# Down-projection weight sums by accumulating DMA, with the final norm out of place

## The chip, the cores and the metric

The kernel runs on one core of one Trainium2 chip, as one program. The metric is the device time of one execution in microseconds (us), given as a median over runs. In the profile the engines are PE (TensorE matmul), PEld (its weight loads), DVE (VectorE), ACT (ScalarE), POOL (GpSimd) and SP (SyncE); SPq is SP's queue of transfers.

## The reference

One decoder layer over 1024 tokens of width 1024 in float32: a mixer with three groups of attention heads, then a gated feed-forward block. The change lies in the last lines only, the down projection, the last norm and the residual:

```python
h = rmsnorm(x, ffn_pre_norm[l])
u = causal_depthwise_conv(h @ w_up[l], conv_w[l], conv_b[l])
gate, up = jnp.split(u, 2, axis=-1)
y = (jax.nn.gelu(gate, approximate=True) * up) @ w_down[l]      # (1024 x 2816) @ (2816 x 1024)
x = x + rmsnorm(y, ffn_post_norm[l])
# rmsnorm(y, g) = y * rsqrt(mean(y*y) + 1e-6) * g
```

## The kernel before

Every float32 product is made of three matmuls: each operand is split into a high part (a cast to float32r on ACT) and the rest (a subtraction on DVE), and high by high, high by rest and rest by high are added in PSUM (`mm3`). A `form` is this split of one operand: one cast on ACT (L935) and one subtraction on DVE (L138) into a tile `wf`.

The down projection is done in 2 x 2 blocks with seven products instead of eight, P1, P2, P7, P5, P6, P3, P4 in this order, each called a pass. A pass runs over 11 pairs `p` of contraction blocks (`ND` = 11); the step for one pair is four row tiles of 128 rows by 512 columns, three matmuls each, so 12 matmuls. Before its step a pair needs two forms: one of the activations (`dg`, read back from `gd` in HBM) and one of the weights (`dwr`, from `w_down`). The passes P7, P5, P6 and P4 need sums of weight blocks: P7 the difference of two blocks, P5 the difference of two others, P6 a block minus the P5 result, P4 a block minus the P6 result. `t_sum` makes these sums on DVE (L906, `dwr<-dwr`), and the sums of P5 and P6 are kept in HBM (`td`) for the passes after.

The order on PE, DVE, ACT and POOL is written by hand: `down_items` is a list of (time, function), sorted by time, with one unit of time for one step, and each engine issues its instructions in this order. SP's order is set by the scheduler from its own estimate of when each transfer may start; SP also issues in order, and a transfer that waits holds up those behind it. In a pass every item leads its step by a fixed number of steps: `w_load` by 4.6, `t_sum` by 2.7, the two forms by 2.2 and 1.8.

After a pass its four PSUM tiles are added into `y` (`evac`). The last pairs of P4 (`TAIL` of them) are ordered by row tile instead of by pair, so that one row tile after another is complete; for each, `evac`, `norm1` and `norm2` follow: DVE adds PSUM to `y`, ACT squares and sums `y` into `dsq`, DVE multiplies `y` by the gain `gff` in place, DVE reduces `dsq` and forms the variance, POOL takes its power -0.5 (L112), DVE scales by it and adds the residual `x2r` (L1282, in two halves), and SP writes the tile out.

Weight tiles of the passes after P1 have the tag `p` with six buffers, shared with the tiles of the phase before.

Of the kernel before, what the change touches and what calls it, by code (L numbers as in the profile page):

```python
# [9 lines left out]
F32 = mybir.dt.float32  # L10
# [3 lines left out]
ALU = mybir.AluOpType  # L14
AX = mybir.AxisListType
# [28 lines left out]
ND = NC2 // 2  # L44
# [3 lines left out]
PB = 6  # L48
# [11 lines left out]
def trunk_kernel(ctx: ExitStack, tc: tile.TileContext, a: dict, out: bass.AP):  # L60

    nc = tc.nc
    V, A, G, T = nc.vector, nc.scalar, nc.gpsimd, nc.tensor

    cst = ctx.enter_context(tc.tile_pool(name="cst", bufs=1))
# [38 lines left out]
    def blk(i, n=P):  # L104
        return slice(i * n, (i + 1) * n)

    def rstd(dst, ssq, n):

        w = ssq.shape[-1]
        v = sm("var", w)  # L110
        V.tensor_scalar(out=v, in0=ssq, scalar1=1.0 / n, scalar2=EPS, op0=ALU.mult, op1=ALU.add)  # L111
        G.tensor_tensor(out=dst, in0=v, in1=mhalf[:, 0:w], op=ALU.pow)  # L112

    def square_sum(dst, src):

# [161 lines left out]
    def step(f, *x):  # L277
        return lambda: f(*x)
# [626 lines left out]
    def tt(eng, out_, x, y, op):  # L905
        eng.tensor_tensor(out=out_, in0=x, in1=y, op=op)  # L906
# [3 lines left out]
    def h2_forms(k2):  # L910

        pairs = {"B11": (0, k2), "B12": (1, k2), "B21": (0, k2 + 2), "B22": (1, k2 + 2)}
        for n, key in pairs.items():
            hB[n, k2] = (h2h[key], h2l[key])
        b11, b12, b21, b22 = (h2r.pop(pairs[n]) for n in ("B11", "B12", "B21", "B22"))
        t1 = S("hf", F32, (P, 2, 512))

        def form(n, x):
            hi, lo = S("hTf", F32R, (P, 2, 512)), S("hTf", F32R, (P, 2, 512))
            A.copy(hi, x)  # L920
            sub(lo, x, hi, V)
# [8 lines left out]
    LO, HI = slice(0, 512), slice(512, 1024)  # L930

    def split(x, eng=None):

        f = S("wf", F32R, (P, 2, 512))
        A.copy(f[:, 0], x)  # L935
        sub(f[:, 1], x, f[:, 0], eng or V)
        return f

    def up_pair(j, at):
# [28 lines left out]
        for n, tm in (("A11", -3.7), ("A12", -2.7), ("S2", -1.7), ("S1", -0.7), ("S3", 0.3), ("S4", 1.6), ("A22", 2.3)):  # L968
            it.append((tm, step(form, n)))
# [172 lines left out]
    for x, i in enumerate(PRE[NAUTO:]):  # L1142
        t0 = 4.0 * (x - NF + NAUTO)
# [33 lines left out]
    def a_of(m, p):  # L1177
        return {"P1": lambda: g1[p][:, LO], "P2": lambda: g2[p][:, LO], "P7": lambda: g1[p][:, LO], "P5": lambda: g1[p][:, HI],
                "P6": lambda: g1[p][:, LO], "P3": lambda: g2[p][:, LO], "P4": lambda: g2[p][:, HI]}[m]()

    def b_of(m, p):
        return wr[m, p][:, HI if m == "P5" else LO]

    def w_load(m, p):
        early = m == "P1"
        t = wr[m, p] = S("dwr", tag="s" if early else "p", bufs=None if early else PB)
        w1, w2 = a["w_down"][p], a["w_down"][ND + p]
        src = {"P1": ((LO, w1[:, LO]),), "P2": ((LO, w2[:, LO]),), "P7": ((LO, w1[:, HI]), (HI, w2[:, HI])),
               "P5": ((slice(0, 1024), w1),), "P6": ((LO, w2[:, HI]), (HI, td[0, p])), "P3": ((LO, w2[:, HI]),),
               "P4": ((LO, w2[:, LO]), (HI, td[1, p]))}[m]  # L1190
        for sl, x in src:
            load(t[:, sl], x)

    def t_sum(m, p):
        t = wr[m, p]
        if m == "P7":
            tt(V, t[:, LO], t[:, HI], t[:, LO], ALU.subtract)
        elif m == "P5":
            tt(V, t[:, HI], t[:, HI], t[:, LO], ALU.subtract)
            load(td[0, p], t[:, HI])  # L1200
        else:
            tt(V, t[:, LO], t[:, LO], t[:, HI], ALU.subtract)
            if m == "P6":
                load(td[1, p], t[:, LO])
# [13 lines left out]
    def form(m, p, side):  # L1218
        forms[m, p, side] = split(b_of(m, p) if side else a_of(m, p))
        if side:  # L1220
            del wr[m, p]
        elif m == "P4":
            del g2[p]

# [43 lines left out]
    def norm1(t, c):  # L1268
        if t not in sqs:
            sqs[t] = cst.tile([P, 2], F32, name=f"dsq{t}")  # L1270
        hs = blk(c, 512)
        square_sum(sqs[t][:, c:c + 1], y[t][:, hs])
        tt(V, y[t][:, hs], y[t][:, hs], env2["g"][:, hs], ALU.mult)

    def norm2(t):
        xt = env2.pop(("x", t))
        s_, r = sm("zs", 1), sm("zr", 1)
        V.tensor_reduce(out=s_, in_=sqs[t], axis=AX.X, op=ALU.add)
        rstd(r, s_, D)
        for c in range(2):  # L1280
            hs = blk(c, 512)
            V.scalar_tensor_tensor(out=y[t][:, hs], in0=y[t][:, hs], scalar=r, in1=xt[:, hs], op0=ALU.mult, op1=ALU.add)  # L1282
            if t == NT - 1:
                load(out[0, blk(t), hs], y[t][:, hs])
        if t < NT - 1:
            load(out[0, blk(t), :], y[t])

    def x_get(t):
        env2["x", t] = S("x2r", tag="pt", bufs=2) if t < 2 else S("x2r")
        load(env2["x", t], x2d[blk(t), :])  # L1290

    TAIL = 3
    down_items = []

    def at_(tm, f, *x):
        down_items.append((tm, step(f, *x)))

    for x, m in enumerate(PASS):
        for p in range(ND):
            t0 = ND * x + p  # L1300
            tf_ = t0
            if x == 6 and p >= ND - TAIL:
                tf_ = ND * x + ND - TAIL + (p - ND + TAIL) / 4
            if m == "P1":
                at_(t0 - 5.6, g_load, p, 0)
            if m == "P2":
                at_(t0 - 6.6, g_load, p, 1)
            at_(tf_ - (5.5 if m == "P1" else 4.6), w_load, m, p)
            if m not in ("P1", "P2", "P3"):
                at_(tf_ - 2.7, t_sum, m, p)  # L1310
            if m == "P2":
                at_(t0 - 1.0, s_sum, "S3", p)
            elif m == "P7":
                at_(t0 - 3.3, s_sum, "S1", p)
            elif m == "P5":
# [122 lines left out]
```

## Time and profile before

| | before |
|---|---|
| median of 3 runs | 1207.08 us (1206.49 to 1207.63) |
| the profiled execution's own time | 1205.29 us |
| its span, first to last instruction | 1203.3 us |
| mean granted TensorE clock in it | 0.983 of full speed |
| PE, DVE, ACT, POOL busy share of the span | 95%, 77%, 48%, 18% |
| transfers | 156.47 MB, all on SP's queue, 39.2% of the 16 engines' span |

The shares are means over a span with many stages. The profiled execution is 1.79 us under the median of the runs, and 1.99 us of its own time lie outside the span.

### The profile page before, as it was taken

Reading aid. Unit: us, or ns where it says so; the run is one execution under the profiler, and the core shown is the slowest. Engines: PE = TensorE matmul, PEld = TensorE weight load, DVE = VectorE, ACT = ScalarE, POOL = GpSimd, SP = SyncE. Lnnn points to the kernel's source line nnn. Section 1 sums busy time; section 2 is a strip of 40 time slices with the busy share of each in tenths; the row PEclk is TensorE's granted clock in tenths of the full one; section 3 lists DMA queues with packets and bytes.
Section 4 is the critical chain, followed back from the end, with each engine's and each line's share of the span. In section 5 each row is a group of like instructions: output and inputs, shape, how many; then the busy total and the mean of one; then the engine's idle time right before and its main releaser. Section 6 shows DMA issues by size and latency. Waiting matters only on the chain.

```text
span 1203.3 us, 15547 instructions
## 1 busy us (share of the span) xinstructions
PE 1142.7 (95%) x5634; PEld 952.3 (79%) x5634; DVE 929.7 (77%) x1422; ACT 581.8 (48%) x1175; POOL 217.2 (18%) x157
## 2 busy tenths in 40 slices
PE   7999989999887999999999999999999999999993
PEld 6977768788776788878888888888888888888872
DVE  6357576765589898762689999989898888896996
ACT  5315543244277777753554434444443455344541
POOL 1100010012077454430001221212122110000000
PEclk9999989999989999999999999999999999999997
DMA  9393224513551222141113212122221489567573
GB/s 345 123 281 89 57 63 159 180 36 106 162 137 36 71 70 87 37 157 35 53 53 123 95 64 105 70 88 83 75 105 59 147 311 340 158 219 249 190 244 140
DMA packets 68462, 156.47 MB, mean 130 GB/s; under 512 B 7169, under 2 KB 23089, under 8 KB 68385
## 3 DMA queue, kind: packets, MB, share of 16 engines
q1 hardware_dynamic: 68384, 155.48, 39.2%
q8 instruction: 44, 0.72, 0.3%
q14 instruction: 34, 0.27, 0.1%
HBM read 116.78 MB, written 37.63 MB: 128 GB/s over the span
## 4 chain that ended last, share of the span: by engine, by line
PE 75%; DVE 13%; DMA 5%; ACT 3%; issue 3%; POOL 1%; SPq 0%; DVEq 0%; POOLq 0%; ACTq 0%
PE p L142 6%; PE p L143 6%; PE p L141 6%; PE scd L620 4%; PE psct L141 3%; PE psct L142 3%; PE psct L143 3%; DVE wf L138 3%; PE xz L142 3%; PE xz L143 3%; PE xz L141 3%; PE accd L653 2%; PE pso L141 2%; PE pso L143 2%; PE pso L142 2%
## 5 line engine op out<-in xcount | busy, mean ns | idle before, releaser
L883 DVE SCALAR_TENSOR_TENSOR u<-C,cw,u 128x1023 f32<-128x1023 f32 (+1 forms) x88 | 112.4, 1279 | 11.5 <-ACT u L880 11.4
L880 ACT ACTIVATE u<-C,cw 128x1024 f32<-128x1024 f32 x44 | 54.8, 1245 | 113.4 <-DVE C L906 88.3
L906 POOL TENSOR_TENSOR sq<-sq,sq 128x512 f32<-128x512 f32 x18 | 29.2, 1622 | 354.5 <-DVE sq L906 354.5
L935 ACT CAST wf<-dwr 128x512 fp32r<-128x512 f32 x77 | 48.0, 623 | 82.1 <-DVE dwr L906 65.0
L141 PE MATMUL p<-h2h,wf 128*128 128x512 f32 x216 | 84.0, 389 | 0.0
L142 PE MATMUL p<-h2l,wf 128*128 128x512 f32 x216 | 84.0, 389 | 0.0
L143 PE MATMUL p<-h2h,wf 128*128 128x512 f32 x216 | 84.0, 389 | 0.0
L653 PE MATMUL accd<-pt,v 128*128 128x256 f32 (+1 forms) x336 | 61.0, 301 | 16.0 <-DVE pt L138 11.6
L630 ACT ACTIVATE pd<-scd,nm 128x128 f32<-128x128 f32 (+3 forms) x64 | 47.5, 743 | 54.4 <-DVE nm L628 49.1
L134 ACT CAST pt<-tpd 128x512 fp32r<-128x512 f32 (+1 forms) x80 | 42.3, 542 | 64.3 <-PE tpd L643 51.6
L141 PE MATMUL psct<-hTh,wh 128*128 128x512 f32 x176 | 69.7, 396 | 0.0
L142 PE MATMUL psct<-hTl,wh 128*128 128x512 f32 x176 | 69.3, 394 | 0.0
L143 PE MATMUL psct<-hTh,wl 128*128 128x512 f32 x176 | 69.0, 392 | 0.0
L653 PEld LDWEIGHTS accd<-pt,v 128*128 128x128 f32 x336 | 50.1, 200 | 22.6 <-DVE pt L138 14.4
L138 DVE TENSOR_TENSOR wf<-wraw,wf 128x512 fp32r<-128x512 f32 x90 | 61.6, 684 | 2.7 <-ACT wf L935 2.7
L138 DVE TENSOR_TENSOR pt<-tpd,pt 128x512 fp32r<-128x512 f32 (+1 forms) x80 | 49.6, 630 | 18.0 <-ACT pt L134 17.6
L138 DVE TENSOR_TENSOR wf<-dwr,wf 128x512 fp32r<-128x512 f32 x77 | 52.7, 685 | 12.8 <-ACT wf L935 12.5
L628 DVE TENSOR_REDUCE nm<-scd 128x1 f32<-128x128 f32 (+3 forms) x64 | 46.9, 750 | 17.7 <-PE scd L620 17.4
L112 POOL TENSOR_TENSOR zr<-var,mhalf 128x1 f32<-128x1 f32 x24 | 13.2, 549 | 260.9 <-DVE var L111 260.9
L141 PE MATMUL xz<-hTf,wf 128*128 128x512 f32 x144 | 56.0, 389 | 0.0
L142 PE MATMUL xz<-hTf,wf 128*128 128x512 f32 x144 | 56.0, 389 | 0.0
L143 PE MATMUL xz<-hTf,wf 128*128 128x512 f32 x144 | 56.0, 389 | 0.0
(291 smaller groups left out, 3502.9 us busy)
## 6 DMA issues: line engine op xcount, KB each, us to landing
wraw<-in_w_up_dram SPq DMA_DIRECT2D x44, 512.0 KB
dwr<-in_w_down_dram SPq DMA_DIRECT2D x77, 256.0 KB
gd<-u SPq DMA_DIRECT2D x22, 512.0 KB
dg<-gd SPq DMA_DIRECT2D x22, 512.0 KB
wraw<-in_wqk_dram SPq DMA_DIRECT2D x11, 512.0 KB
dwr<-in_w_down_dram SPq DMA_DIRECT2D x11, 512.0 KB
td<-dwr SPq DMA_DIRECT2D x22, 256.0 KB
dwr<-td SPq DMA_DIRECT2D x22, 256.0 KB
```

The lines of the kernel that those rows point to most:

```text
L134: A.copy(dst, src)
L138: (eng or G).tensor_tensor(out=dst, in0=x, in1=hi.bitcast(F32), op=ALU.subtract)
L141: T.matmul(ps, lhsT=lh, rhs=rh, start=start, stop=False)
L142: T.matmul(ps, lhsT=lh, rhs=rl, start=False, stop=False)
L143: T.matmul(ps, lhsT=ll, rhs=rh, start=False, stop=stop)
L620: T.matmul(sc[:, off + c0:off + c1], lhsT=ql[0:rows, blk(i)], rhs=kl[0:rows, c0:c1], start=x == 0, stop=x == len(passes) - 1)
L628: V.tensor_reduce(out=nm, in_=s, axis=AX.X, op=ALU.max, negate=True)
L630: A.activation(p[:, 0:n], s, AF.Exp, bias=nm, accum_out=den[:, i, hd["d"]:hd["d"] + 1])
L653: T.matmul(acc[:, cs], lhsT=hd["v"][:, j], rhs=pt[:, x, bs], start=j == 0 and x == 0, stop=d == 1 and x == 1 and (o == len(ops) - 1 or (o ...
L880: A.activation(us[i], ct2[i], AF.Identity, bias=cw[:, i, 3:4], scale=cw[:, i, 2:3])
L883: V.scalar_tensor_tensor(out=us[i][:, d:], in0=ct2[i][:, 0:SEQ - d], scalar=cw[:, i, 2 - d:3 - d], in1=us[i][:, d:], op0=ALU.mult, op1=ALU ...
L935: A.copy(f[:, 0], x)
```

## The change

Weights: a tile `dwr` now holds one block for each of two pairs of steps (512 columns each), so six buffers hold twelve pairs. A sum is no longer made on DVE. The first block is loaded, in P7 and P5 ACT multiplies it by -1 in place (`w_neg`, L1193), and a transfer issued by POOL adds the second block onto it in SBUF (`w_add`, L1197, `accum_op`). P7's sum goes to `td` by SP; P6 starts from it, and after its form ACT negates it and SP stores it for P4 (`w_keep`). The loads of P7, P5, P6 and P4 lead by 7.6 steps, the negations by 6.0, the accumulating transfers by 5.6.

Norm: the product with the gain goes to a new tile `yg` instead of back into `y`; the reduction and the power (`norm_r`) are apart from the last scaling (`norm2`), and stand earlier in the list.

Tail: `TAIL` is 4, so the last four pairs are ordered by row tile.

```diff
     def b_of(m, p):
-        return wr[m, p][:, HI if m == "P5" else LO]
+        return wr[m, p // 2][:, blk(p % 2, 512)]
...
+        load(b_of(m, p), {"P1": w1[:, LO], "P2": w2[:, LO], "P7": w1[:, HI], "P5": w1[:, LO], "P6": td[0, p],
+                          "P3": w2[:, HI], "P4": td[1, p]}[m])
+
+    def w_neg(m, p):
+        A.mul(b_of(m, p), b_of(m, p), -1.0)
+
+    def w_add(m, p):
+        w1, w2 = a["w_down"][p], a["w_down"][ND + p]
+        G.dma_start(out=b_of(m, p), in_={"P7": w2[:, HI], "P5": w1[:, HI], "P6": w1[:, LO], "P4": w2[:, LO]}[m],
+                    accum_op=ALU.add)
         if m == "P7":
-            tt(V, t[:, LO], t[:, HI], t[:, LO], ALU.subtract)
...
+            load(td[0, p], b_of(m, p))
+
+    def w_keep(p):
+        w_neg("P6", p)
+        load(td[1, p], b_of("P6", p))
...
+        if (t, 2) not in y:
+            y[t, 2] = S("yg")
         square_sum(sqs[t][:, c:c + 1], y[t][:, hs])
-        tt(V, y[t][:, hs], y[t][:, hs], env2["g"][:, hs], ALU.mult)
+        tt(V, y[t, 2][:, hs], y[t][:, hs], env2["g"][:, hs], ALU.mult)
...
-    TAIL = 3
+    TAIL = 4
...
-            at_(tf_ - (5.5 if m == "P1" else 4.6), w_load, m, p)
+            at_(tf_ - (5.5 if m == "P1" else 4.6 if m in ("P2", "P3") else 7.6), w_load, m, p)
+            if m in ("P7", "P5"):
+                at_(tf_ - 6.0, w_neg, m, p)
             if m not in ("P1", "P2", "P3"):
-                at_(tf_ - 2.7, t_sum, m, p)
+                at_(tf_ - 5.6, w_add, m, p)
...
-                at_(t0 + 5.2, s_sum, "S4", p)
+                at_(t0 - 1.2, s_sum, "S4", p)
...
-                at_(e0 + 0.07, norm2, t + 4)
+                at_(e0 + 0.3, norm_r, t + 4)
+                at_(e0 + 0.6 if t == 3 else e0 + 1.12, norm2, t + 4)
```

On POOL the change shows at the end of its program. The lines are one piece of the difference; `sq` and `C` belong to the phase before, `zr` and `dr` are the powers of the final norm.

```order
-L906 TENSOR_TENSOR sq_8717<-sq_8717,sq_8780 128x512
-L906 TENSOR_TENSOR C<-sq_8780 128x512
-L112 TENSOR_TENSOR zr<-var,mhalf 128x1 x8
-L1434 UNCONDITIONAL_BRANCH
-L1434 ISA
+L906 TENSOR_TENSOR sq_8717<-sq_8717,sq_8779 128x512
+L906 TENSOR_TENSOR C<-sq_8779 128x512
+L1197 DMA dwr<-in_w_down_dram 128x512 x44
```

POOL now issues 44 accumulating transfers between its last sums of the phase before and the eight powers.

On SP, the transfers of the passes P7 and P5 in the changed kernel: `dwr_9329` and `dwr_9380` are the tiles of P7's pairs 6 to 9, `dwr_9431` that of its pair 10, and `dwr_9455` and `dwr_9501` those of P5's pairs 0 to 3.

```order
L97 DMA dwr_9329<-in_w_down_dram 128x512 x2
L97 DMA dwr_9380<-in_w_down_dram 128x512 x2
L97 DMA td_5934<-dwr_9186 128x512
L97 DMA dwr_9431<-in_w_down_dram 128x512
L97 DMA td_5934<-dwr_9186 128x512
L97 DMA td_5934<-dwr_9233 128x512 x2
L97 DMA td_5934<-dwr_9280 128x512
L97 DMA dwr_9455<-in_w_down_dram 128x512 x2
L97 DMA td_5934<-dwr_9280 128x512
L97 DMA td_5934<-dwr_9329 128x512 x2
L97 DMA td_5934<-dwr_9380 128x512 x2
L97 DMA dwr_9501<-in_w_down_dram 128x512 x2
```

The stores of P7's sums, each of which waits for its accumulating transfer, now stand between P7's loads and those of P5.

On DVE, the last two row tiles at the end of the program, before the change:

```order
L906 TENSOR_TENSOR y_9641<-dt_10449,y_9641 128x512
L906 TENSOR_TENSOR y_9641<-y_9641,gff_9889 128x512
L1278 TENSOR_REDUCE zs_10731<-dsq6_10355 128x1
L111 TENSOR_SCALAR var_10734<-zs_10731 128x1
L1282 SCALAR_TENSOR_TENSOR y_9641<-y_9641,zr_10732,x2r_10658 128x512 x2
L906 TENSOR_TENSOR y_9650<-dm_10454,y_9650 128x512
```

The same place after the change (`yg_10348` belongs to the tile before the last, `yg_10398` to the last):

```order
L906 TENSOR_TENSOR y_9645<-dt_10440,y_9645 128x512
L906 TENSOR_TENSOR yg_10348<-y_9645,gff_9883 128x512
L1290 SCALAR_TENSOR_TENSOR yg_10297<-yg_10297,dr5_10680,x2r_10590 128x512 x2
L1282 TENSOR_REDUCE zs_10704<-dsq6_10347 128x1
L111 TENSOR_SCALAR var_10707<-zs_10704 128x1
L906 TENSOR_TENSOR y_9654<-dm_10445,y_9654 128x512
L906 TENSOR_TENSOR yg_10398<-y_9654,gff_9883 128x512
L1290 SCALAR_TENSOR_TENSOR yg_10348<-yg_10348,dr6_10705,x2r_10628 128x512 x2
```

Between a tile's variance and its scaling there now stand the first two operations of the next tile, and between those two and the next tile's reduction the scaling of the tile before.

## Rows read from the trace of the kernel before

**Rows 1.** The page: span and engines.

```profile
span 1203.3 us, 15547 instructions
PE 1142.7 (95%) x5634; PEld 952.3 (79%) x5634; DVE 929.7 (77%) x1422; ACT 581.8 (48%) x1175; POOL 217.2 (18%) x157
```

**Rows 2.** Engines by stretch: P1, P2, P7, P5, P6, P3, P4, then the rest.

```profile
core 0: us, PE busy (x) PEld busy (x) DVE busy (x) ACT busy (x) POOL busy (x), PEclk, DMA share, GB/s
971.20:1001.10 29.90, 29.83 (x131) 24.35 (x131) 22.82 (x33) 18.29 (x32) 0.00 (x0) 1.00 0.98 369
1001.10:1031.00 29.90, 29.90 (x133) 24.76 (x132) 24.15 (x40) 12.75 (x24) 0.00 (x0) 1.00 0.70 246
1031.00:1061.00 30.00, 30.00 (x134) 24.82 (x134) 27.51 (x47) 13.91 (x26) 0.00 (x0) 1.00 0.67 200
1061.00:1090.90 29.90, 29.90 (x134) 24.75 (x133) 25.00 (x42) 13.78 (x26) 0.00 (x0) 1.00 0.69 222
1090.90:1120.80 29.90, 29.52 (x130) 24.13 (x129) 23.38 (x39) 15.06 (x31) 0.00 (x0) 1.00 0.72 236
1120.80:1150.73 29.93, 29.93 (x133) 24.77 (x132) 28.85 (x49) 14.70 (x30) 0.00 (x0) 1.00 0.64 198
1150.73:1188.36 37.63, 32.56 (x133) 25.58 (x131) 32.11 (x61) 13.72 (x30) 2.74 (x5) 0.95 0.63 216
1188.36:1203.30 14.94, 0.00 (x1) 0.00 (x0) 7.96 (x17) 1.44 (x4) 1.65 (x3) 0.65 0.30 119
```

**Rows 3.** Waits of PE from 970 us to the end: total us, times, longest.

```profile
PE dt L142 <- DVE wf L138: 5.5, 4, 2.7
```

**Rows 4.** Timeline of PE in P4: start us, duration, instruction, idle before it.

```profile
1150.73 0.39 PE L141 MATMUL dt<-wf 128*128 128x512 f32 x1
...
1153.45 0.39 PE L141 MATMUL dt<-wf 128*128 128x512 f32 x1
...
1168.99 0.50 PE L142 MATMUL dt<-wf 128*128 128x512 f32 x1 [1.55 <-DVE wf L138]
...
1177.41 0.50 PE L142 MATMUL dt<-wf 128*128 128x512 f32 x1 [2.68 <-DVE wf L138]
...
1179.21 0.79 PE L142 MATMUL dt<-wf 128*128 128x512 f32 x1 [0.84 <-DVE wf L138]
...
1187.97 0.39 PE L143 MATMUL dm<-wf 128*128 128x512 f32 x1
```

**Rows 5.** Timeline of DVE: one whole row tile of the tail, and its last operation.

```profile
1186.61 0.68 DVE L906 TENSOR_TENSOR y<-dm,y 128x512 f32<-128x512 f32 x1
1188.15 0.69 DVE L906 TENSOR_TENSOR y<-y,gff 128x512 f32<-128x512 f32 x1 [0.85 <-ACT junk L119]
1188.76 0.15 DVE L1278 TENSOR_REDUCE zs<-dsq 128x1 f32<-128x2 f32 x1
1188.94 0.15 DVE L111 TENSOR_SCALAR var<-zs 128x1 f32<-128x1 f32 x1
1189.82 1.41 DVE L1282 SCALAR_TENSOR_TENSOR y<-y,zr,x2r 128x512 f32<-128x512 f32 x2 [0.73 <-POOL zr L112]
1191.15 0.68 DVE L906 TENSOR_TENSOR y<-dt,y 128x512 f32<-128x512 f32 x1
...
1198.89 1.42 DVE L1282 SCALAR_TENSOR_TENSOR y<-y,zr,x2r 128x512 f32<-128x512 f32 x2 [0.73 <-POOL zr L112]
```

**Rows 6.** The tile dwr from 980 us on: instructions, count, duration ns min/median/max.

```profile
L906 DVE TENSOR_TENSOR dwr<-dwr x44: 680/684/692, 1016.3 to 1175.5; 128x512 f32<-128x512 f32 x44
L97 SPq DMA_DIRECT2D td<-dwr x22: 326/382/424, 1051.8 to 1125.9; - x22
L97 SPq DMA_DIRECT2D dwr<-td x22: 417/424/474, 1074.8 to 1160.2; - x22
```

**Rows 7.** ACT from 1031 to 1150.73 us: busy us, mean ns, idle before.

```profile
L935 ACT CAST wf<-dwr 128x512 fp32r<-128x512 f32 x43 | 26.8, 622 | 57.4 <-DVE dwr L906 44.4 <-DMA dwr<-in_w_down_dram 10.5 <-PE dx L143 1.6
```

**Rows 8.** Waits of SP's queue from 1031 us on: total us, times, longest.

```profile
SPq L97 <- DMA td<-dwr: 50.5, 17, 4.7
```

More of the change, by code (lines that the diff above doesn't have):

```diff
@@ L1181, in b_of @@
     def b_of(m, p):
-        return wr[m, p][:, HI if m == "P5" else LO]
+        return wr[m, p // 2][:, blk(p % 2, 512)]
     def w_load(m, p):
-        early = m == "P1"
-        t = wr[m, p] = S("dwr", tag="s" if early else "p", bufs=None if early else PB)
+        if (m, p // 2) not in wr:
+            early = m == "P1"
+            wr[m, p // 2] = S("dwr", tag="s" if early else "p", bufs=None if early else PB)
         w1, w2 = a["w_down"][p], a["w_down"][ND + p]
[L1188 to L1195, printed above, removed]
-        if m == "P7":
-            tt(V, t[:, LO], t[:, HI], t[:, LO], ALU.subtract)
[L1198 to L1204, printed above, removed]
+        load(b_of(m, p), {"P1": w1[:, LO], "P2": w2[:, LO], "P7": w1[:, HI], "P5": w1[:, LO], "P6": td[0, p],
[6 more added lines that the diff above has]
+                    accum_op=ALU.add)
+        if m == "P7":
+            load(td[0, p], b_of(m, p))
+    def w_keep(p):
+        w_neg("P6", p)
+        load(td[1, p], b_of("P6", p))
     def s_sum(m, p):
@@ L1220, in form @@
         if side:
-            del wr[m, p]
+            if m == "P6":
+                w_keep(p)
+            if p % 2 or p == ND - 1:
+                del wr[m, p // 2]
         elif m == "P4":
@@ L1271, in norm1, with norm_r, norm2 @@
         hs = blk(c, 512)
+        if (t, 2) not in y:
+            y[t, 2] = S("yg")
         square_sum(sqs[t][:, c:c + 1], y[t][:, hs])
-        tt(V, y[t][:, hs], y[t][:, hs], env2["g"][:, hs], ALU.mult)
-    def norm2(t):
-        xt = env2.pop(("x", t))
-        s_, r = sm("zs", 1), sm("zr", 1)
+        tt(V, y[t, 2][:, hs], y[t][:, hs], env2["g"][:, hs], ALU.mult)
+    def norm_r(t):
+        s_, r = sm("zs", 1), cst.tile([P, 1], F32, name=f"dr{t}")
         V.tensor_reduce(out=s_, in_=sqs[t], axis=AX.X, op=ALU.add)
         rstd(r, s_, D)
+        sqs[t] = r
+    def norm2(t):
+        xt, yg = env2.pop(("x", t)), y.pop((t, 2))
         for c in range(2):
             hs = blk(c, 512)
-            V.scalar_tensor_tensor(out=y[t][:, hs], in0=y[t][:, hs], scalar=r, in1=xt[:, hs], op0=ALU.mult, op1=ALU.add)
+            V.scalar_tensor_tensor(out=yg[:, hs], in0=yg[:, hs], scalar=sqs[t], in1=xt[:, hs], op0=ALU.mult, op1=ALU.add)
             if t == NT - 1:
-                load(out[0, blk(t), hs], y[t][:, hs])
+                load(out[0, blk(t), hs], yg[:, hs])
         if t < NT - 1:
-            load(out[0, blk(t), :], y[t])
+            load(out[0, blk(t), :], yg)
     def x_get(t):
@@ L1346, in trunk_kernel @@
         at_(e6 + 1.6 + 1.6 * t, norm1, t, 1)
-        at_(e6 + 2.2 + 1.6 * t, norm2, t)
+        at_(e6 + 2.2 + 1.6 * t, norm_r, t)
+        at_(e6 + 2.9 + 1.6 * t, norm2, t)
         at_(e6 - 4 + 1.6 * t, x_get, t)
```

## The prediction

> **What bounds the kernel now.** I read the page first: PE is busy for 95% of the span [rows 1]. So a gain needs PE idle time, or time after PE's last matmul. Only the down phase is changed, so I then read it pass by pass [rows 2]. From P1 to P3 PE is busy in nearly all of each stretch: the reader should see that DVE, though it has up to 28.85 us of work in 29.93 us, holds PE up nowhere there. The waits of PE say the same: from 970 us to the end they come to 5.5 us in four waits, all for a weight form made by DVE [rows 3]. The timeline places three of them in the last 20 us [rows 4]. A step starts 2.72 us after the one before (1150.73 to 1153.45), so P4's eleven steps, begun at 1150.73, would end at 1150.73 + 11 x 2.72 = 1180.65. The last matmul starts at 1187.97, and matmuls start 0.23 us apart, so PE is done at 1188.20: it loses 7.55 us, 5.07 in the three waits shown, the rest in restarting and at a lower granted clock (mean 0.95 in this stretch, a mix of the two levels 2.4 and 1.2 GHz, after PE stood idle).
>
> What follows is a chain on DVE. One row tile takes it from 1186.61 to 1191.15, 4.54 us [rows 5]: adding PSUM, 0.85 us of waiting for ACT's sum of squares, the product with the gain, reduction and variance, 0.73 us of waiting for POOL's power, two halves of scaling. A row tile takes PE 9 matmuls, 2.04 us, so DVE falls behind, and ends at 1198.89 + 1.42 = 1200.31, 12.1 us after PE. Writing out takes the last 3.0 us to 1203.3.
>
> **What the change does to the tail.** It takes 44 sums from DVE [rows 6], each 0.61 us from start to start (1188.15 to 1188.76 in [rows 5]), 26.8 us in all. Before P3's end this gives PE nothing. In P4 it removes 11 x 0.61 = 6.7 us from the engine that PE waits for there.
>
> I lay DVE's work after P3's end out again in its new order. Up to the first tail tile it has 17 form subtractions, 4 additions from PSUM and 4 products with the gain, 25 x 0.605 = 15.1 us; four pairs of scalings at 1.33 (1189.82 to 1191.15), 5.3; four reductions with variance at 0.36, 1.4; and about 0.9 of waits for POOL, since between variance and scaling there stand one form, one form, four forms and nothing. That is 22.7 us; begun at 1151.1 it ends at 1173.8. The last form is done 18.7 us in, at 1169.8. PE's first tail tile begins after seven steps, at 1169.8, and needs the last pair's form for its last three matmuls at 1171.8. So forms arrive 2 us in time, PE does not wait, and is done at 1180.7.
>
> PE's first tail tile is complete after eight steps, at 1172.5, and DVE is there at 1173.8. A tail tile now costs DVE 0.6 + 0.6 + 1.33 + 0.36 = 2.9 us: ACT's squares lie beside the product, which no longer overwrites their input, and POOL's power lies beside the next tile's two operations. Addition and product wait for one another without ACT (0.1 us a tile). First tile 1.54 + 0.36; three more 3 x 2.9; last power 0.7; last scaling 1.4; hand-overs 0.4: 13.1 us, ending at 1186.9. With the same 3.0 us of writing the span is 1189.9, against 1203.3: 13.4 us less, 7.5 of it on PE and 5.9 after it.
>
> The larger `TAIL` alone lets four forms fall due within one tile instead of three; the cover is the 2 us above. Were it gone, PE would wait and the end would move one for one. The extra tiles `yg` need buffers that hold `wf` otherwise; no row prices this, and a form that waits for a buffer shows as PE waiting for DVE.
>
> **What it does to the transfers.** ACT gets 33 negations. I price one as a cast, 0.62 us [rows 7]: 6.8 us more in P7, where ACT has 13.91 of 30.00 [rows 2], so it fits. But ACT is in order: a negation whose load is late holds the casts behind it.
>
> The accumulating transfers are the unknown: no row shows one, nor any transfer issued by POOL. Bytes give a lower bound. A plain 256 KB takes all engines 0.70 us at P1's rate (369 GB/s at share 0.98) and 0.88 us at P7's (200 at 0.67) [rows 2]; I use 0.79. An accumulating one reads the source, reads the destination and writes it. If it costs as one plain transfer it is 0.79; as two, 1.58; as three of the slow kind, 2.64. I take two, nearest to a transfer whose read side carries twice the bytes.
>
> Is there room? P7, P5 and P6 have 33 loads, 22 stores and 33 accumulations in 33 steps, 89.8 us. The plain ones take 55 x 0.79 = 43.5. P2's stretch has share 0.70, so 9.0 us of it are free for loading ahead, for which twelve pairs in six buffers leave room. That leaves (89.8 + 9.0 - 43.5) / 33 = 1.68 us for each accumulation. At 1.58 it fits, narrowly; at 0.79 easily. P3 has only loads, and share 0.64 now, so P4 can run ahead.
>
> Time to land matters as well as throughput. From `w_add` to the weight cast there are 5.6 - 1.8 = 3.8 steps, 10.3 us. SP's stores wait for the accumulation, and loads for P5 stand behind them, as SP already waits 50.5 us for stores to `td` [rows 8] at no cost to PE. For the landing of a POOL-issued transfer only a page has a price: the Trainium skill (DMA: Bandwidth & Descriptors, Anatomy of one DMA) puts it at 2.0 us plus the bytes at 436 GB/s, as an estimate 2.6 us here without the added read; by that the sum stays as it is, and no row here shows it.
>
> **The sum.** 13.4 us less than the profiled execution's 1205.29 is 1191.9; the median of the runs stood 1.79 us above that, so I forecast 1207.08 - 13.4 = 1193.7, rounded to 1194.
>
> **The rivals.**
> - *The transfers become the bound (slower).* Above 1.68 us an accumulation, the DMA engines in P7 to P6 fall behind and PE waits 33 times the excess. At 2.64 that is 31.7 us: 1194 + 31.7 = 1225.7. The gain is used up at 1.68 + 13.4 / 33 = 2.09 us. For it: my middle value lies only 0.1 below the point where waiting begins, and no row shows such a transfer. Against it: share 0.67 to 0.72 in these passes now, with the same bytes written.
> - *A late link (smaller gain).* Load, negation, accumulation and store wait for one another in P7 and P5, through in-order ACT, POOL and SP. If landing under load exceeds 10.3 us by 2 us for each of P5's six buffers, of which half falls on PE, that is 6 us: 1200. For it: P5's loads stand behind P7's stores. Against it: 3.8 steps of lead. At twice the excess, 12 us, little or nothing is left: 1206, no change.
> - *POOL's issue is starved by DVE (slower).* If POOL could write a transfer's descriptors only while DVE is idle, each accumulation would have what DVE leaves: 89.8 - 75.9 us of busy time in P7 to P6 [rows 2] + 33 x 0.68 of removed sums = 36.3 us, 1.1 us each. An issue that needed twice that would cost 33 x 1.1 = 36 us: 1230. Against it: POOL gets 217.2 us of work done in this kernel beside a DVE that is busy for 77% of it [rows 1], so it is not shut out. The Trainium skill (SBUF — State Buffer, sections "SBUF: two separate sides" and "Who interferes with whom") states such a lock, but for DVE's two-port modes, and says that `tensor_tensor` has none and was not seen to stall a DMA; by its first statement alone this rival would hold, by both the forecast; no row here has a POOL-issued transfer to test it.
> - *The tail does not shorten.* If forms still arrive late in P4 (a buffer, or an accumulation), PE keeps its 7.5 us and only the 5.9 behind it are gained: 1201.
>
> **How the numbers follow.** Forecast 0.66, with its own range 1191 to 1198; late link or tail on PE, still faster, 0.08; no change 0.05; transfers as the bound 0.18; starved issue 0.03. Within 0.2% (2.4 us) a measurement of this kernel cannot tell a change from none. So faster 0.74, same 0.05, slower 0.21. The range goes from 1190 (DVE not behind at the first tail tile, 1.3 us, and fewer hand-overs) to 1212, an accumulation of 2.2 us; what lies beyond is most of the two slow cases.
>
> **What would show it.** Right: no wait of PE from 970 us on, its last matmul near 1180; DVE's row tiles about 2.9 us apart in the tail with no wait for ACT and one for POOL; span near 1190. Wrong: PE waiting for DVE forms whose ACT cast waits for a `dwr` transfer in P7 to P6, with a DMA share near 1 (the transfers as the bound) or well below it (the late link or the starved issue); or PE's waits again only in P4 (the tail).

## The result and the profile after

| | before | after |
|---|---|---|
| median of the runs | 1207.36 us (1206.49 to 1212.58, 4 runs) | 1192.86 us (1191.09 to 1194.75, 4 runs) |
| ratio, 95% interval | | 0.9871 [0.9838, 0.9904] |
| span of the profiled execution | 1203.3 us | 1190.1 us |
| mean granted TensorE clock | 0.983 | 0.981 |

The changed kernel is faster by 1.3%, 14.5 us by the medians. The same kernel sent again beside the first experiments gave 1192.98 us and 0.9875 [0.9847, 0.9904]. The forecast was 1194. One profiled execution further down, that of the kernel with five pairs by row tile, ran at a mean granted clock of 0.747 and took 1434.92 us, so neither its trace nor its time is used.

The line of the page of after that answers to [rows 1], then those of its two kinds of queues (packets, MB, share of 16 engines' span):

```profile
PE 1145.4 (96%) x5634; PEld 956.5 (80%) x5634; DVE 903.5 (76%) x1378; ACT 598.8 (50%) x1208; POOL 257.5 (22%) x201
...
q1 hardware_dynamic: 63632, 143.95, 35.6%
q0 software_dynamic: 6336, 11.54, 5.5%
```

PE does the same work in a shorter span; DVE has lost 44 instructions, ACT has gained 33. Of the bytes of these two queues 7% have moved to POOL's (q0). The passes of after from P2 on, P2, P7, P5, P6, P3, P4, then the rest, against [rows 2]:

```profile
core 0: us, PE busy (x) PEld busy (x) DVE busy (x) ACT busy (x) POOL busy (x), PEclk, DMA share, GB/s
1001.50:1031.40 29.90, 29.90 (x134) 24.75 (x133) 21.70 (x37) 22.78 (x43) 9.18 (x11) 1.00 1.08 323
1031.40:1061.40 30.00, 30.00 (x134) 24.83 (x133) 20.77 (x35) 13.09 (x25) 6.77 (x8) 1.00 0.94 261
1061.40:1091.40 30.00, 30.00 (x134) 24.84 (x133) 20.22 (x33) 16.75 (x31) 13.21 (x15) 1.00 0.93 216
1091.40:1121.40 30.00, 30.00 (x134) 24.86 (x133) 23.09 (x37) 22.67 (x47) 0.00 (x0) 1.00 0.65 198
1121.40:1151.30 29.90, 29.90 (x134) 24.75 (x133) 25.31 (x43) 14.32 (x31) 9.82 (x11) 1.00 0.92 214
1151.30:1181.30 30.00, 30.00 (x134) 24.65 (x132) 27.25 (x54) 11.88 (x28) 4.48 (x6) 1.00 0.51 181
1181.30:1190.10 8.80, 0.18 (x1) 0.00 (x0) 4.89 (x11) 0.72 (x2) 1.10 (x2) 0.80 0.45 179
```

The reader is to see three things. P4 now takes 30.0 us like every other pass, at clock 1.00; before it took 37.6 at 0.95. The rest after PE is 8.8 us, not 14.94. And the DMA share has risen from 0.67 to 0.94 in P7 while PE stayed full; the view of PE's waits has no row after 960 us. The tail on DVE, against [rows 5]:

```profile
1167.99 1.29 DVE L138 TENSOR_TENSOR wf<-dwr,wf 128x512 fp32r<-128x512 f32 x2
...
1173.45 0.68 DVE L906 TENSOR_TENSOR y<-dt,y 128x512 f32<-128x512 f32 x1
...
1176.08 0.69 DVE L906 TENSOR_TENSOR y<-dm,y 128x512 f32<-128x512 f32 x1 [0.75 <-PE dm L143]
...
1178.99 0.68 DVE L906 TENSOR_TENSOR y<-dt,y 128x512 f32<-128x512 f32 x1
1179.71 0.69 DVE L906 TENSOR_TENSOR yg<-y,gff 128x512 f32<-128x512 f32 x1
1180.32 1.41 DVE L1290 SCALAR_TENSOR_TENSOR yg<-yg,dr,x2r 128x512 f32<-128x512 f32 x2
1181.64 0.15 DVE L1282 TENSOR_REDUCE zs<-dsq 128x1 f32<-128x2 f32 x1
...
1181.89 0.68 DVE L906 TENSOR_TENSOR y<-dm,y 128x512 f32<-128x512 f32 x1
...
1185.55 1.42 DVE L1290 SCALAR_TENSOR_TENSOR yg<-yg,dr,x2r 128x512 f32<-128x512 f32 x2 [0.66 <-POOL dr L112]
```

From 1178.99 to 1181.89 a row tile takes 2.90 us and waits for nobody; before it took 4.54 with two waits. Of the four tiles of the tail only the last still waits for POOL.

The transfers at L1197 in after: instruction time in ns (min/median/max), and the time from issue to landing:

```profile
L1197 POOL DMA_DIRECT2D dwr<-in_w_down_dram x44: 875/875/1937, 1010.4 to 1145.1; - x44
...
DMA to landing us min/median/max: 3.7/7.7/12.0
```

### The profile page after: what moved, and what is told of

It is laid out like the page before. It is cut to its first block, busy times and chain, and to the rows that moved or that the text cites. A ratio compares the mean times of both kernels' runs of the same rounds, so it can differ in the third digit from the quotient of the medians.

```text
span 1190.1 us, 15581 instructions
## 1 busy us (share of the span) xinstructions
PE 1145.4 (96%) x5634; PEld 956.5 (80%) x5634; DVE 903.5 (76%) x1378; ACT 598.8 (50%) x1208; POOL 257.5 (22%) x201
## 4 chain that ended last, share of the span: by engine, by line
PE 84%; DVE 7%; DMA 3%; ACT 3%; issue 2%; SPq 0%; POOL 0%; DVEq 0%; POOLq 0%; ACTq 0%
PE p L141 6%; PE p L143 6%; PE p L142 6%; PE scd L620 4%; PE psct L142 3%; PE psct L141 3%; PE psct L143 3%; PE xz L141 3%; PE xz L143 3%; PE xz L142 3%; PE dx L142 3%; PE dx L141 3%; PE dx L143 3%; PE accd L653 2%; PE pso L141 2%; PE pso L143 2%
## 5 line engine op out<-in xcount | busy, mean ns | idle before, releaser
L653 PE MATMUL accd<-pt,v 128*128 128x256 f32 (+1 forms) x336 | 62.3, 306 | 15.1 <-DVE pt L138 10.3
L1197 POOL DMA_DIRECT2D dwr<-in_w_down_dram x44 | 39.0, 987 | 136.2 <-ACT dwr L1193 76.8
L138 DVE TENSOR_TENSOR wf<-dg,wf 128x512 fp32r<-128x512 f32 x77 | 54.1, 702 | 10.3 <-ACT wf L935 10.3
```

The source lines that it names most:

```text
L138: (eng or G).tensor_tensor(out=dst, in0=x, in1=hi.bitcast(F32), op=ALU.subtract)
L653: T.matmul(acc[:, cs], lhsT=hd["v"][:, j], rhs=pt[:, x, bs], start=j == 0 and x == 0, stop=d == 1 and x == 1 and (o == len(ops) - 1 or (o ...
L1197: G.dma_start(out=b_of(m, p), in_={"P7": w2[:, HI], "P5": w1[:, HI], "P6": w1[:, LO], "P4": w2[:, LO]}[m], accum_op=ALU.add)
```

## The experiments

The part before the down phase is the same in all these kernels, yet the down phase begins between 968.8 and 976.5 us from one execution to the next. So beside each time stand parts of the profiled execution, counted from the first matmul of the down phase: PE until its last matmul ends (its start and 0.23 us, the distance between two matmuls), DVE after that until its last instruction ends, then writing until the end of the span (us).

| kernel | median | ratio to before | PE | DVE after | writing | sum |
|---|---|---|---|---|---|---|
| before | 1207.36 | | 218.07 | 12.11 | 2.99 | 233.17 |
| after | 1192.86 | 0.9871 [0.9838, 0.9904] | 209.85 | 5.65 | 3.13 | 218.63 |
| after, again | 1192.98 | 0.9875 [0.9847, 0.9904] | 209.83 | 5.65 | 3.11 | 218.59 |
| E1 norm alone | 1202.12 | 0.9942 [0.9922, 0.9962] | 216.25 | 6.93 | 4.30 | 227.48 |
| E2 sums alone | 1200.20 | 0.9925 [0.9906, 0.9945] | 209.85 | 12.31 | 3.11 | 225.27 |
| E3 three pairs | 1194.84 | 0.9893 [0.9867, 0.9919] | 209.85 | 6.94 | 3.82 | 220.61 |
| E4 no accumulating | 1192.86 | 0.9876 [0.9845, 0.9907] | 209.83 | 5.63 | 3.16 | 218.62 |
| E5 twice as many | 1227.42 | 1.0170 [1.0138, 1.0203] | 240.22 | 7.93 | 4.48 | 252.63 |
| E6 short leads | 1215.47 | 1.0048 [1.0024, 1.0073] | 230.34 | 6.66 | 3.14 | 240.14 |
| E7 last tile first | 1193.48 | 0.9890 [0.9860, 0.9920] | 209.83 | 5.11 | 3.83 | 218.77 |
| E8 five pairs | 1193.00 | 0.9887 [0.9863, 0.9910] | - | - | - | - |
| E9 halves | 1191.58 | 0.9884 [0.9857, 0.9910] | 209.85 | 5.11 | 3.02 | 217.98 |
| E10 late negation | 1216.96 | 1.0082 [1.0059, 1.0104] | 228.89 | 6.12 | 3.16 | 238.17 |
| E11 late addition | 1200.29 | 0.9948 [0.9928, 0.9968] | 218.38 | 5.89 | 3.11 | 227.38 |

The runs of before beside E1 to E3 and the repetition had a median of 1209.45 us, those beside E4 to E7 1207.41, those beside E8 to E11 1206.76.

### E1: the norm alone

The kernel before, with the new `norm1`, `norm_r` and `norm2`; sums stay on DVE, `TAIL` stays 3.

```diff
-        tt(V, y[t][:, hs], y[t][:, hs], env2["g"][:, hs], ALU.mult)
+        tt(V, y[t, 2][:, hs], y[t][:, hs], env2["g"][:, hs], ALU.mult)
...
-                at_(e0 + 0.07, norm2, t + 4)
+                at_(e0 + 0.3, norm_r, t + 4)
+                at_(e0 + 0.6 if t == 3 else e0 + 1.12, norm2, t + 4)
...
-        at_(e6 + 2.2 + 1.6 * t, norm2, t)
+        at_(e6 + 2.2 + 1.6 * t, norm_r, t)
+        at_(e6 + 2.9 + 1.6 * t, norm2, t)
```

> The kernel before with the norm out of place and split alone; sums of weights still on DVE, last three pairs by row tile. Theory: DVE still carries the 11 sums of P4 (6.7 us), so PE still waits for forms, 2.5 us or more in P4, and DVE reaches the first tail tile near 1180.5; from there 13.1 us on DVE (2.9 us a tile, no wait for ACT) and 3.0 us of writing: span about 1197, 6.5 us under before. Rival (the gain is all behind PE, the transfers bring nothing): span about 1190 already here. Rival (the norm's order brings nothing, only DVE's relief does): span 1203, as before.

It gave 5.7 us from the first matmul of the down phase on, 5.2 of them behind PE and 1.8 on PE, against 1.3 more for writing. PE still waits in P4 (total, times, longest, from 965 us on):

```profile
PE dt L142 <- DVE wf L138: 3.0, 2, 2.2
```

So the norm alone shortens the tail, but with the sums DVE still has too much to do before P4's last forms.

### E2: the sums alone

The changed kernel with the old norm, in place and in its old places, and `TAIL` 3.

```diff
-        tt(V, y[t, 2][:, hs], y[t][:, hs], env2["g"][:, hs], ALU.mult)
+        tt(V, y[t][:, hs], y[t][:, hs], env2["g"][:, hs], ALU.mult)
...
-    TAIL = 4
+    TAIL = 3
...
-                at_(e0 + 0.3, norm_r, t + 4)
-                at_(e0 + 0.6 if t == 3 else e0 + 1.12, norm2, t + 4)
+                at_(e0 + 0.07, norm2, t + 4)
```

> The changed kernel with the norm as before (in place, reduction and scaling together) and the last three pairs by row tile: the accumulating transfers alone. Theory: DVE's last form comes 6.7 us earlier than before, PE does not wait and is done near 1181; DVE then takes four tiles of 4.54 us from about 1175.4, ending at 1193.7, and 3.0 us of writing: span about 1197, 6.5 us under before. Rival (the gain is all in the norm's order): span 1203. Rival (the transfers alone carry the gain): span 1190.

PE has no wait and its whole gain, 8.22 us; behind PE nothing is gained (12.31 against 12.11). A row tile of its tail on DVE:

```profile
1176.85 0.69 DVE L906 TENSOR_TENSOR y<-dt,y 128x512 f32<-128x512 f32 x1 [0.55 <-PE dt L143]
1178.39 0.69 DVE L906 TENSOR_TENSOR y<-y,gff 128x512 f32<-128x512 f32 x1 [0.85 <-ACT junk L119]
...
1180.07 1.41 DVE L1285 SCALAR_TENSOR_TENSOR y<-y,zr,x2r 128x512 f32<-128x512 f32 x2 [0.73 <-POOL zr L112]
1181.40 0.68 DVE L906 TENSOR_TENSOR y<-dm,y 128x512 f32<-128x512 f32 x1
```

The two waits of [rows 5] are there again, with the same numbers, and the tile takes the same time, 1181.40 - 1176.85 = 4.55 us. So the parts have their own shares: moving the sums gives PE's, the norm gives what lies behind PE. With the sums E2 also takes over what goes with them in the change, the tiles that hold two pairs, the longer leads and the earlier place of one sum of activations (`S4`); no run has these apart.

### E3: three pairs by row tile instead of four

```diff
-    TAIL = 4
+    TAIL = 3
```

> The changed kernel with the last three pairs by row tile instead of four. Theory: forms are in time in either case, so PE runs through; the first tail tile is complete at 1174.5 instead of 1172.5, but DVE is not free before 1173.8, and its scaling of the last tile but one now stands beside the last power of POOL, which gives 0.5 us back: span 1190 to 1191, no difference that can be measured from the changed kernel. Rival (the fourth pair is what lets DVE start early): 2 us longer, 1192.

PE is at 209.85 us with either. Behind it E3 is 2.0 us longer, so the rival held. 1.29 of it are on DVE, which gets its first complete row tile later: with three pairs a row tile takes PE 9 matmuls, about 2.04 us, and DVE 3.13 (1181.30 to 1184.43), so DVE falls back with each. The other 0.69 are in writing, where the last two tiles' scalings come back to back, as in E7 below.

```profile
1181.30 0.69 DVE L906 TENSOR_TENSOR y<-dt,y 128x512 f32<-128x512 f32 x1
...
1184.43 0.69 DVE L906 TENSOR_TENSOR y<-dm,y 128x512 f32<-128x512 f32 x1
...
1186.24 2.74 DVE L1290 SCALAR_TENSOR_TENSOR yg<-yg,dr,x2r 128x512 f32<-128x512 f32 x4
```

The trace shows it; the times cannot (0.9893 against 0.9875, intervals overlap).

### E4: the same transfers without accumulating

```diff
-        G.dma_start(out=b_of(m, p), in_={"P7": w2[:, HI], "P5": w1[:, HI], "P6": w1[:, LO], "P4": w2[:, LO]}[m],
-                    accum_op=ALU.add)
+        G.dma_start(out=b_of(m, p), in_={"P7": w2[:, HI], "P5": w1[:, HI], "P6": w1[:, LO], "P4": w2[:, LO]}[m])
```

> The changed kernel with POOL's 44 transfers as plain copies that overwrite their destination instead of adding to it, so the sums of weights are left out and the output is not the reference's. Theory: the read of the destination is what makes an accumulating transfer cost 1.49 us of all engines (5.5% of 1190.1 us over 44); without it the price is that of a plain transfer, 0.75 to 0.80 us, issue on POOL stays at 0.88 us, landing becomes shorter than 7.7 us; the time stays at 1192 to 1194 since all of it is hidden. Rival (POOL's issue or DVE beside it sets the price): price and landing stay as they are.

Nothing moves, 218.62 us against 218.63: in the changed kernel the accumulation is wholly hidden. But its price can now be read: POOL's queue on E4's page first, then its transfers.

```profile
q0 software_dynamic: 3520, 11.54, 2.9%
```

```profile
L1197 POOL DMA_DIRECT2D dwr<-in_w_down_dram x44: 548/548/771, 1013.3 to 1147.7; - x44
...
DMA to landing us min/median/max: 2.8/4.9/6.7
```

A plain transfer takes all engines 2.9% x 1192.1 / 44 = 0.79 us; an accumulating one, by the page of after, 5.5% x 1190.1 / 44 = 1.49 us, 1.9 times as much. It has 144 packets instead of 80, takes POOL 0.875 us to issue instead of 0.548 (expected was no difference), and lands after 7.7 us instead of 4.9.

### E5: every accumulating transfer twice

Each `w_add` is followed by a second transfer of the same block, added onto spare tiles that nothing reads, four blocks in turn.

```diff
...
+        G.dma_start(out=spare[spare[4] % 4], in_={"P7": w2[:, HI], "P5": w1[:, HI], "P6": w1[:, LO], "P4": w2[:, LO]}[m],
+                    accum_op=ALU.add)
+        spare[4] += 1
```

> The changed kernel with each accumulating transfer issued a second time onto a spare tile that nothing reads. Theory (room for 1.68 us an accumulation in P7 to P6, 1.49 used): at 2.98 PE waits 33 x 1.3 = 43 us, by the free share that the changed kernel's trace leaves there (14 us of 49 needed) 35 us; time 1225 to 1237, PE waiting for forms in P7 to P6 at a DMA share near 1. Rival (the transfers are far from a bound): no wait of PE, 1192 to 1195. Rival (it is landing time and not throughput that counts): PE waits, but at a share well under 1.

1227.42 us: with doubled transfers the change would be a loss. POOL's queue on its page, then stretches from P7 on, then what ACT waits for from 1020 to 1180 us:

```profile
q0 software_dynamic: 12672, 23.07, 10.3%
```

```profile
1033.40:1070.00 36.60, 35.70 (x156) 28.66 (x155) 20.91 (x34) 15.74 (x28) 16.27 (x19) 1.00 1.10 261
1070.00:1105.00 35.00, 31.27 (x121) 21.69 (x120) 18.99 (x30) 15.62 (x28) 17.50 (x20) 1.00 1.11 246
1105.00:1140.00 35.00, 30.22 (x113) 20.12 (x111) 20.44 (x32) 20.29 (x39) 10.55 (x12) 1.00 1.09 258
```

```profile
ACT wf L935 <- DMA dwr<-in_w_down_dram: 57.0, 33, 3.0
```

The DMA engines are the bound here: their share stays at 1.09 to 1.11 for over 100 us while PE has gaps, and ACT's casts wait for transfers. POOL, too, now waits before many transfers until an earlier one has landed, on a spare block or in `dwr`; but the engines are not idle meanwhile: by the trace's packets, 16 or more were on the 16 engines at once for 96 to 99% of each of these stretches. Counted by matmuls (132 to a pass), P7 to P6 take 110.4 us instead of 89.8, P3 is undisturbed, and P4 loses 9.8. One doubled step costs 2 x 1.44 = 2.88 us of all engines, so in P7 to P6 there is room for 2.88 - 20.6 / 33 = 2.26 us a step.

### E6: short leads

Loads, negations and additions lead as loads and `t_sum` did before.

```diff
-            at_(tf_ - (5.5 if m == "P1" else 4.6 if m in ("P2", "P3") else 7.6), w_load, m, p)
+            at_(tf_ - (5.5 if m == "P1" else 4.6 if m in ("P2", "P3") else 4.6), w_load, m, p)
             if m in ("P7", "P5"):
-                at_(tf_ - 6.0, w_neg, m, p)
+                at_(tf_ - 3.1, w_neg, m, p)
             if m not in ("P1", "P2", "P3"):
-                at_(tf_ - 5.6, w_add, m, p)
+                at_(tf_ - 2.7, w_add, m, p)
```

> The changed kernel with the leads of before: loads 4.6 steps ahead, negations 3.1, accumulating transfers 2.7. Theory: from the transfer's place to the form there are 0.9 steps, 2.4 us, against a landing of 3.7 to 12.0 us (median 7.7); forms in P7 and P5 come late, PE waits some us in each of the two passes; time 1195 to 1205. P6 and P4 have no negation and are not affected. Rival (the lead in the list is not what sets the transfer's start): no wait of PE, 1192 to 1194.

A miss: the kernel is slower than before, 20.5 us more on PE than after, 14.0 of them in P7 to P6 and 6.5 in P4. Its stretches in P7 and P5, then ACT's wait from 1033 to 1066 us:

```profile
1033.40:1066.00 32.60, 30.51 (x134) 24.72 (x133) 17.23 (x28) 13.29 (x24) 7.47 (x9) 1.00 0.83 203
1066.00:1098.00 32.00, 26.33 (x103) 18.59 (x102) 17.06 (x27) 16.88 (x31) 8.44 (x11) 1.00 0.71 154
```

```profile
ACT wf L935 <- DMA dwr<-in_w_down_dram: 16.2, 5, 6.9
```

Here the DMA share is well below that of E5 and still PE stands: transfers are late, not too many. My reading, put to the test in E10 and E11, was a ring of in-order engines: ACT's negation late, so POOL's addition, so SP's store of the sum, so the loads queued on SP behind that store, so ACT's next casts and negations.

### E10: late negation, early loads

```diff
             if m in ("P7", "P5"):
-                at_(tf_ - 6.0, w_neg, m, p)
+                at_(tf_ - 3.1, w_neg, m, p)
             if m not in ("P1", "P2", "P3"):
-                at_(tf_ - 5.6, w_add, m, p)
+                at_(tf_ - 2.7, w_add, m, p)
```

> The changed kernel with loads at 7.6 steps as in it, but negations at 3.1 and accumulating transfers at 2.7 steps ahead. Theory (the place of the negation in ACT's order sets when POOL may start, and with it SP's stores and the loads behind them): about as slow as with all three leads short, 1205 to 1218. Rival (the loads' place in SP's order did it): no loss, 1192 to 1195.

1216.96 us, the same loss as E6 although loads lead by 7.6 steps again: P7 to P6 lose 11.8 us, P4 7.2. So the loads' lead is not what E6 lost by in the main (the 2.2 us that E6 loses more in P7 to P6 stay open). ACT's waits for transfers from 1020 to 1180 us, then stretches of ACT and of POOL in P5:

```profile
ACT wf L935 <- DMA dwr<-in_w_down_dram: 51.0, 19, 8.1
```

```profile
1062.61 0.63 ACT L1193 ACTIVATE dwr<-dwr 128x512 f32<-128x512 f32 x1
...
1068.75 0.62 ACT L935 CAST wf<-dwr 128x512 fp32r<-128x512 f32 x1 [2.49 <-DMA dwr<-in_w_down_dram]
...
1069.80 0.62 ACT L1193 ACTIVATE dwr<-dwr 128x512 f32<-128x512 f32 x1
```

```profile
1063.53 0.87 POOL L1197 DMA_DIRECT2D dwr<-in_w_down_dram  x1 [2.42 <-ACT dwr L1193]
...
1070.72 0.88 POOL L1197 DMA_DIRECT2D dwr<-in_w_down_dram  x1 [3.29 <-ACT dwr L1193]
```

The trace shows a shorter ring than the one that I had read. A negation (1062.61) lets POOL start its transfer (1063.53); the cast of that pair waits for it (1068.75); the negation of the pair two further on stands behind that cast in ACT's order (1069.80), and with it POOL's next transfer but one (1070.72). A turn, two steps, takes 7.19 us here, where PE at full speed needs 5.44. SP is no link of it: none of the 33 negations of E10, or of E6, waits for a transfer, so their loads were there in time.

### E11: late addition alone

```diff
             if m not in ("P1", "P2", "P3"):
-                at_(tf_ - 5.6, w_add, m, p)
+                at_(tf_ - 2.7, w_add, m, p)
```

> The changed kernel with only the accumulating transfers' place moved from 5.6 to 2.7 steps ahead, loads and negations as in it. Theory: POOL does nothing else there and starts each transfer when its negation and load are done, whatever its place in the list; no difference, 1192 to 1195, no wait of PE in P7 to P6. Rival (the place of the transfer counts): several us longer, like the run with short leads.

P7 to P6 lose nothing, 89.8 us as in after, and the trace says why: there the transfers start when they do in after, counted from the first matmul of the down phase within 0.4 us in P7 and P5 and 0.9 in P6. POOL has nothing else to do in these passes and waits for the negation, whatever the transfer's place in the list, as expected. P7's last transfer in after, then in E11, 59.70 and 59.68 us after that matmul:

```profile
1031.17 0.88 POOL L1197 DMA_DIRECT2D dwr<-in_w_down_dram  x1 [1.84 <-ACT dwr L1193]
```

```profile
1029.90 0.87 POOL L1197 DMA_DIRECT2D dwr<-in_w_down_dram  x1 [1.85 <-ACT dwr L1193]
```

So what E10 lost in P7 to P6 came from the negation's place; how late a transfer itself could start there E11 does not test. But PE loses 8.5 us in P4, which I had not expected. POOL in P4, then ACT, then PE's waits:

```profile
1155.40 0.94 POOL L112 TENSOR_TENSOR dr<-var,mhalf 128x1 f32<-128x1 f32 x1 [18.98 <-DVE var L111]
1156.30 1.77 POOL L1197 DMA_DIRECT2D dwr<-in_w_down_dram  x2
1163.42 0.56 POOL L112 TENSOR_TENSOR dr<-var,mhalf 128x1 f32<-128x1 f32 x1 [5.35 <-DVE var L111]
1163.94 3.55 POOL L1197 DMA_DIRECT2D dwr<-in_w_down_dram  x4
```

```profile
1160.53 0.62 ACT L935 CAST wf<-dwr 128x512 fp32r<-128x512 f32 x1 [8.50 <-DMA dwr<-in_w_down_dram]
```

```profile
PE dt L141 <- ACT wf L935: 2.9, 3, 1.7
```

P4's additions now stand behind the norm's powers in POOL's order, and POOL waits 18.98 and 5.35 us for DVE's variances. The transfers behind leave late, ACT's casts wait for them, PE for the casts. PE's recorded waits are only 2.9 of the 8.5 us; from 1175 to 1180 us, between and behind them, the granted clock is 0.50, 1.2 GHz, and matmuls there start 0.43 us apart instead of 0.23. In after the last addition is issued at 1145.1, ahead of the first power at 1156.67. E6 and E10 have their additions as late in the list, and POOL's order in their P4 is the same, with waits of 19.14 and 15.86 us before the first power; so their losses in P4 are of this kind.

### E7: the last tile ahead of the scaling before it

```diff
-                at_(e0 + 0.6 if t == 3 else e0 + 1.12, norm2, t + 4)
+                at_(e0 + (0, 1.12, 1.12, 1.32, 0.6)[t + 1], norm2, t + 4)
```

> The changed kernel with the scaling of the last tile but one moved behind the last tile's variance, so that it lies beside POOL's last power. Theory: of the 0.66 us for which DVE waits there some 0.5 us are saved, span 1189.6 against 1190.1, too little for the times to tell. Rival (ACT's last sum of squares then comes too late): nothing is saved.

DVE ends 0.54 us earlier, 5.11 after PE, and the gain is lost in writing, 3.83 for 3.13 us: the last two tiles' scalings now come back to back, so the 512 KB write of the one starts close before the two 256 KB writes of the other. That this closeness is the cause was argued until E9.

### E8: five pairs, and halves

E9's edit with other places for the scalings and one pair more.

```diff
-    TAIL = 4
+    TAIL = 5
...
-                at_(e0 + 0.6 if t == 3 else e0 + 1.12, norm2, t + 4)
+                at_(e0 + (0, 1.37, 1.37, 1.57, 0.6)[t + 1], norm2, t + 4)
```

> The changed kernel with the last five pairs by row tile, the last scaling but one beside POOL's last power, and the last four tiles written out in halves as soon as a half is scaled. Theory: in the changed kernel DVE waits 0.75 us for PE at the second tail tile, so an earlier first tile is worth at most that; the reordering saved DVE 0.54 us before and gave 0.7 back in writing, which the halves should return; from the first matmul of the down phase to the end 217 to 218 us against 218.6. Rival (forms fall due too early with five pairs): PE waits in P4 and it is longer. The times can hardly tell either from the changed kernel.

0.9887 [0.9863, 0.9910], not to be told from after. With no trace in hand nothing is said of where its time goes.

### E9: E7, with the last four tiles written by halves

```diff
-            if t == NT - 1:
+            if t >= 4:
                 load(out[0, blk(t), hs], yg[:, hs])
-        if t < NT - 1:
+        if t < 4:
             load(out[0, blk(t), :], yg)
```

> The same without the fifth pair: reordering and halves alone. Theory: DVE ends 0.5 us earlier after PE (5.1 instead of 5.65) and writing takes 3.1 us again instead of 3.8: 218.1 us from the first matmul of the down phase. Rival (writing is bound by the bytes of the last two tiles, not by when each is issued): writing stays at 3.8 and nothing is gained.

Writing is back at 3.02 us with DVE's end at 5.11, together 217.98, 0.65 less than after. Its last instructions on DVE are E7's order, four halves in a row:

```profile
1181.04 2.74 DVE L1290 SCALAR_TENSOR_TENSOR yg<-yg,dr,x2r 128x512 f32<-128x512 f32 x4
```

So E7's loss was in how the tiles before the last are written; E9 changes three of them at once. The median, 1191.58, is the lowest of all, but 0.9884 [0.9857, 0.9910] does not set it apart from after.

## Why the prediction was right

**PE.** Forecast: 7.5 us in P4, as P4 would run its eleven steps at 2.72 us. P4 began at 1151.40 and PE ended at 1181.32, which is 29.92 = 11 x 2.72; before it took 37.47, so 7.55 were gained. Another 0.67 was gained ahead of P4, mostly in P6, where [rows 2] has 29.52 of 29.90; I had left it out. E2 shows that moving the sums, with what goes with it, is sufficient for all of it, E1 that the norm alone recovers 1.8 of it.

**Behind PE.** Forecast 5.9, measured 6.46, and writing 0.14 more. The size of a row tile was right: 2.9 us forecast, 2.90 measured. The course was somewhat different from what I laid out. I had DVE 1.3 us behind PE at the first tail tile; it was there 1.0 us ahead of the forecast (P4's later start taken off), and waited 0.75 us for PE at the second. With four pairs a row tile takes PE 12 matmuls, 2.72 us, close to DVE's 2.90. So DVE stays near PE, begins its last tile 0.57 us after PE's end, and then there remains one tile's chain, 5.08 us. This explains E3 as well.

**The forms in P4** were forecast to be done at 1169.8; they were at 1169.28, and PE did not wait. Buffers for `yg` held nothing up.

**The transfers.** Forecast 1.58 us of all engines for an accumulating transfer, measured 1.49 with 0.79 for a plain one, so "two plain ones" was nearly right; no row had shown it, and to have taken the middle of three prices was in part luck. The room was mis-sized: 1.68 us in the sum, 2.26 by E5. I had let the engines' share end at 1; it stands at 1.09 to 1.11 where they are the bound (and at 1.08 in after's P2, where additions run ahead). With 1.10 put in for 1, my sum gives 2.04; the remaining 0.22 stays open. The rival of transfers as the bound was therefore farther off than its 0.18 said, but its mechanism is real: E5 is that case.

**Late link.** Not in after: some transfers took longer than the 10.3 us that I gave them, up to 12.0, but PE waited for none. Those 10.3 us were a distance in the list and not one in time, since ACT runs ahead of the list: P5's eighth transfer starts at 1063.71 and its cast at 1070.00, 6.3 us later. That a late link costs PE time is shown by E10, 11.8 us in P7 to P6; that this is near the 12 at which I saw the gain used up is chance, as those 12 were worked out from landing, and what came late in E10 was the negation. Of the links that I named, ACT and POOL are in E10's ring, and SP's stores and loads are not. And one queue was not in my prediction at all: POOL's own in P4, where an addition can fall behind the norm's powers (8.5 us in E11). That the changed kernel keeps clear of both by its leads was nowhere worked out.

**Starved issue.** Not so: the issue took 0.875 us at the median, while DVE was busy for 20 to 22 of each 30 us in P2, P7 and P5, mostly with operations on two tensors. The longest, 1.937, is one of several issues that start 0.55 us apart. The Trainium skill (SBUF — State Buffer, "Who interferes with whom") says that such operations did not stall transfers, while modes with two ports do; the trace agrees with the first, and no run here shows the second.

**The total.** Forecast 13.4 us off the span, measured 13.2; from the down phase's first matmul on it is 14.54. The difference, 1.34 us, is what the unchanged part took more in that execution. So the down phase gained 1.1 us more than forecast, in P6 and behind PE, and that the span agrees within 0.2 us is in part luck.

## What to carry to other kernels

Work that is moved off the engine that PE waits for pays in full only in the stage where PE waits; here 44 sums were moved, and nearly all of PE's gain lies in the last pass, which has 11 of them (no run moved these 11 alone). A place in a list is not a time: an engine that has nothing else to do starts when its input is there, wherever the item stands (E11 in P7 to P6), and one that has other work in its queue waits behind it (E11 in P4). So when a chain crosses several in-order engines, ask for each link what it waits for and what stands before it in its queue (E10). A transfer that accumulates cost the DMA engines here about two plain ones, and hides as long as that fits.

## What was not expected of the hardware

The DMA share of the trace is not capped at 1: with transfers as the bound it stood at 1.09 to 1.11 (E5).

An accumulating transfer of 256 KB from POOL landed after 7.7 us, a plain one after 4.9 (E4; the least were 3.7 and 2.8). The Trainium skill (DMA: Bandwidth & Descriptors, Anatomy of one DMA), by which I had estimated 2.6 us, is near the least and well short of the median in this stretch, where the DMA share was 0.92 to 1.08 in the four passes in which they were issued.

POOL's power, a 128x1 operation, took 0.55 us in most places and 0.93 to 1.04 in others. The timeline of after has both:

```profile
1161.04 0.69 DVE L138 TENSOR_TENSOR wf<-dwr,wf 128x512 fp32r<-128x512 f32 x1
...
1161.19 0.95 POOL L112 TENSOR_TENSOR dr<-var,mhalf 128x1 f32<-128x1 f32 x1 [3.59 <-DVE var L111]
...
1182.06 0.55 POOL L112 TENSOR_TENSOR dr<-var,mhalf 128x1 f32<-128x1 f32 x1 [2.35 <-DVE var L111]
```

It is long beside a DVE operation with both tensors in SBUF (1161.04), short beside one that reads PSUM (the addition at 1181.89) or beside an idle DVE; all eight of before, where DVE waits for them, take 0.55. One power breaks the pattern, 0.88 us beside an idle DVE in E5, right behind the issue of a transfer. The DVE operation beside it keeps its 0.69. The Trainium skill (SBUF — State Buffer, "Who interferes with whom") has the rule, that a DVE instruction with two inputs in SBUF contends with a GpSimd instruction that reads SBUF; these rows agree, though no run isolates it. Here it costs up to 0.46 us of waiting for DVE at a time (the scalings at 1157.64 and 1162.17 in after), and PE nothing.
